# A hybrid decoder block: more matrix products by seven, two weight sums added by DMA, gate rows spread over two sweeps

## The chip, the cores and the metric

The kernel runs on one core of a Trainium2 chip. The metric is the device time of one execution in microseconds (us). The core has TensorE (matmuls, PE in the profile, with its weight loads as PEld), VectorE (DVE), ScalarE (ACT), GpSimd (POOL) and SyncE (SP), which issues nearly all transfers; 16 DMA engines move the bytes.

## The reference

One decoder block on 512 tokens of width 2048, in float32: adaLN modulation, an input projection, an RWKV-7 mixer beside a pooling mixer, an output projection, then a gated MLP with a causal convolution of width 3, and a final norm. What the change touches is the MLP and its last gate:

```python
def _conv_ffn(h, w_up, conv_w, conv_b, w_down):
    u = h @ w_up                                   # 2048 -> 2 * 5632
    up = jnp.pad(u, ((0, 0), (CONV_WIDTH - 1, 0), (0, 0)))
    y = conv_b
    for j in range(CONV_WIDTH):
        y = y + conv_w[j] * up[:, j:j + T]
    val, gate = jnp.split(y, 2, axis=-1)
    return (jax.nn.silu(gate) * val) @ w_down      # 5632 -> 2048

mod = c_act @ w_ada[l] + b_ada[l]
sh1, sc1, gt1, sh2, sc2, gt2 = jnp.split(mod[:, None, :], N_MOD, axis=-1)
...
x = x + gt2 * _conv_ffn(h, w_up[l], conv_w[l], conv_b[l], w_down[l])
```

## The kernel before, in words

Everything is held with features on the 128 partitions and the 512 tokens along the free dimension. A float32 product is made of three matmuls in a faster format: each operand is split into a high and a low part, and `mm3` does high x high, high x low and low x high (lines 121 to 123). ScalarE makes the high part by a cast, VectorE the low part by a difference. `split_weights` does so for a weight slice of 512 columns: it loads it into a `wraw` buffer (4 of them), casts to `whi`, subtracts to `wlo` (3 buffers, lines 113 to 117). `project` runs a row of such slices.

The program is traced in written order and ordered by a planner: it simulates the engines with estimated costs, gives each engine a fixed order of instructions, and lets a ready instruction go ahead of one written earlier that is not ready. Buffers are handed out in that simulated order too. On the chip each engine and each queue then runs its own list strictly in order and waits where data or a buffer is missing.

The MLP's inner width is 44 tiles of 128, and each comes as a pair, a value and a gate column block. Pairs 0 to 4 are done ordinarily. The next 26 pairs (`NSEV`) use a seven-product scheme on 2 x 2 blocks (value and gate, two halves of the tokens, two halves of the 2048 inputs). The inputs of a pair are cut into four chunks (`NPC`), and for each chunk the kernel loads four blocks of the weights (`load_four`, 512 KB), forms four sums of them on GpSimd (`weight_sums`: lines 956, 957, 958; the first writes two sums at once), splits three blocks and four sums into high and low parts (`parts`, lines 968 and 969: tiles ph, pl for the blocks, sh, sl for the sums, two buffers of each) and does seven products of six matmuls, each on half of the tokens: 42 matmuls of 128 x 256. Sums lie in buffers shared with the ordinary weights: two sums in a `wraw`, two in a `wlo`. The first three products use the blocks, the last four the sums. After the fourth chunk `combine` (lines 983 to 990) makes value and gate from the seven results; `gated` runs the convolution (lines 836 to 838), the gating (842, 843) and stores the tile to `actd`.

The 13 pairs that are left are done ordinarily, as a list of 104 quarters (`plain_tiles`): a quarter is one weight slice of 512 columns and 12 matmuls of 128 x 512, and every eighth ends a pair. One quarter is put between the two groups of products of each chunk from the third on; what remains runs after the last chunk.

The down projection then runs in two sweeps: eight output tiles at a time over all 44 inner tiles, four at a step. `act_tiles` loads and splits four tiles of `actd` (line 1065, 143, 144), and eight calls of `down` follow, each one weight slice and 12 matmuls. The last eight inner tiles of the second sweep are done by token halves together with the final norm. Before the down stage, 16 tiles of the residual are reloaded (line 1054) into a pool that takes the place of the up stage's own pool.

The gate of the MLP, 16 columns of the modulation, is computed on VectorE: `ada_gate2` loads a broadcast of a quarter of the activated `c` (line 1081) and rows of `w_ada` (256 KB each, line 1084, two buffers), and one VectorE instruction a row multiplies and sums (line 1085). 64 rows are needed, 16 columns times four quarters. They come in groups of eight, one group at each of steps 1 to 8 of the first sweep; at step 9 the quarters are added (lines 1094 to 1097).

Of the kernel before, what the change touches and what calls it, by code (L numbers as in the profile page):

```python
# [1 line left out]

# [1 line left out]

# [5 lines left out]
F32 = mybir.dt.float32  # L10
# [3 lines left out]
ALU = mybir.AluOpType  # L14
PSUM = bass.MemoryType.PSUM

P = 128
T = 512
D = 2048
KT = D // P  # L20
NF = 44
# [7 lines left out]
NB = 8  # L29
Q = float(np.exp(-0.5))  # L30
WINS = (2, 4, 8, 16)
NORD = 5
NSEV = 26
NPC = 4
DK = 4

# [26 lines left out]
def block_kernel(ctx, tc, a, out, stop=None, dbg=None):  # L63
    nc = tc.nc
    V, S, G, PE = nc.vector, nc.scalar, nc.gpsimd, nc.tensor
# [23 lines left out]
    def cols(name, lo, hi):  # L89
        return vec[:, COLS[name] + lo : COLS[name] + hi]  # L90
# [11 lines left out]
    mod = cp.tile([P, 96], F32, tag="mod", name="mod")  # L102
# [3 lines left out]
    V.tensor_scalar_add(b1p, cols("b_ada", 16, 32), 1.0)  # L106

    mark = [None, None]

    def split_weights(src, eng=V):  # L110
        w = src.shape[-1]
        raw = wp.tile([P, WC], F32, tag="wraw", name="wraw", bufs=4)
        nc.sync.dma_start(raw[:, 0:w], src)
        hi = wp.tile([P, WC], F32R, tag="whi", name="whi", bufs=3)
        mark[0] = S.copy(hi[:, 0:w], raw[:, 0:w]).ins  # L115
        lo = wp.tile([P, WC], F32R, tag="wlo", name="wlo", bufs=3)
        mark[1] = eng.tensor_tensor(lo[:, 0:w], raw[:, 0:w], hi[:, 0:w].bitcast(F32), op=ALU.subtract).ins  # L117
        return hi, lo

    def mm3(ps, wh, wl, xh, xl, start, stop):  # L120
        PE.matmul(ps, wh, xh, start=start, stop=False)  # L121
        PE.matmul(ps, wh, xl, start=False, stop=False)  # L122
        return PE.matmul(ps, wl, xh, start=False, stop=stop)  # L123

    def project(ps, src, acts, start=True, stop=True, engs=(V,)):

        n = len(acts)
        for k0 in range(0, n, WC // P):
            nk = min(WC // P, n - k0)
            wh, wl = split_weights(src[:, k0 * P : (k0 + nk) * P], engs[k0 // 4 % len(engs)])  # L130
            for kk in range(nk):
                k = k0 + kk
                sl = slice(kk * P, (kk + 1) * P)
                last = mm3(ps, wh[:, sl], wl[:, sl], *acts[k], start=start and k == 0, stop=stop and k == n - 1)
        return last

    def slots(k, tag="a"):
# [34 lines left out]
    cact = tc.dram_tile([1, D], F32, name="cact")  # L172
# [3 lines left out]
    first = {}  # L176
    p0ctx = ExitStack()
    p0 = p0ctx.enter_context(tc.tile_pool(name="p0", bufs=1))
    if True:
        cb = p0.tile([P, D], F32, tag="cb", name="cb")  # L180
# [29 lines left out]
        for k in range(KT):  # L210
# [7 lines left out]
            hi, lo = slots(k)  # L218
# [26 lines left out]
        for k in range(KT):  # L245
# [3 lines left out]
            hi, lo = slots(k)  # L249
# [465 lines left out]
    for g in range(NQ):  # L715
# [9 lines left out]
        if g < NQ - 1:  # L725
            win_some(pairs, (0, 2))
            with tc.high_priority(offset=50000):
                r, k = load_cells(g + 1, (0, 1))
# [50 lines left out]
    rb = ctx.enter_context(tc.tile_pool(name="rb", bufs=1, reuse_waits="tile"))  # L779
# [118 lines left out]
    upctx, up = stage("up")  # L898
# [33 lines left out]
    for j in range(2, NORD):  # L932
        tiles = []
        for i in range(2):
            ps = bank()
            last = project(ps, a["wup"][2 * j + i - 4, :, :], H2)
# [8 lines left out]

    W2 = 2 * P

    def load_four(n):
        raw = up.tile([P, 4, W2], F32, tag="raw", name="raw", bufs=2)
        nc.sync.dma_start(raw, a["wups"][n // NPC, n % NPC, :, :, :])  # L950
        return raw

    def weight_sums(raw):
        sa = wp.tile([P, WC], F32, tag="wraw", name="sums", bufs=4)[:, :].rearrange("p (n w) -> p n w", n=2)
        sb2 = wp.tile([P, WC], F32, tag="wlo", name="sums", bufs=3)[:, :].rearrange("p (n w) -> p n w", n=2)
        G.tensor_tensor(sa, raw[:, 1:3, :], raw[:, 0:1, :].to_broadcast([P, 2, W2]), op=ALU.add)  # L956
        G.tensor_tensor(sb2[:, 0, :], sa[:, 0, :], raw[:, 2, :], op=ALU.add)  # L957
        G.tensor_tensor(sb2[:, 1, :], sb2[:, 0, :], raw[:, 3, :], op=ALU.add)
        return sa, sb2

    def parts(tag, srcs):
        m = sum(t.shape[1] for t in srcs)
        hi = up.tile([P, m, W2], F32R, tag=tag + "h", name=tag + "h", bufs=2)
        lo = up.tile([P, m, W2], F32R, tag=tag + "l", name=tag + "l", bufs=2)
        n = 0
        for t in srcs:
            sl = slice(n, n + t.shape[1])
            act = S.copy(hi[:, sl, :], t)  # L968
            dve = V.tensor_tensor(lo[:, sl, :], t, hi[:, sl, :].bitcast(F32), op=ALU.subtract)  # L969
            n += t.shape[1]  # L970
        return [(hi[:, i, :], lo[:, i, :]) for i in range(m)], (act, dve)
# [21 lines left out]
    def plain_tiles():  # L993
        for j in range(NORD + NSEV, NF):
            yv = None
            for i in range(2):
                ps = bank()
                for k0 in range(0, KT, WC // P):
                    k1 = k0 + WC // P
                    project(ps, a["wup"][2 * (j - NSEV) + i - 4, :, k0 * P : k1 * P], H2[k0:k1],  # L1000
                            start=k0 == 0, stop=k1 == KT)
# [6 lines left out]

    NST = NSEV * NPC
    others = plain_tiles()  # L1010
    raws = [load_four(0), load_four(1)]
    sums = weight_sums(raws[0])
    pw, _ = parts("p", [raws[0][:, 1:4, :]])
    q = {}
    for n in range(NST):
        c = n % NPC
        if n + 1 < NST:
            raw = raws.pop()
            nsums = weight_sums(raw)
            npw, marks = parts("p", [raw[:, 1:4, :]])  # L1020
            if n + 2 < NST:
                raws.append(load_four(n + 2))
        with tc.issue_after(marks[0].ins), tc.issue_after(marks[1].ins):
            sw, _ = parts("s", sums)
        (a22, a11, a12), (s1, s3, s2, s4) = pw, sw
        ks = (2 * c, 2 * c + 1)
        b11, b21, b22 = half([H2[k] for k in ks], 0), half([H2[k + HK] for k in ks], 0), half([H2[k + HK] for k in ks], 1)
        t1, t2, t3, t4 = ([TK[k][i] for k in ks] for i in range(4))
        if c == 0:
            q = {}  # L1030
        for m, w, xs_ in ((1, a11, b11), (2, a12, b21), (4, a22, t4)):
            if c == 0:
                q[m] = bank()[:, 0:HT]
            product(q[m], c, w, xs_)
        if n >= 2:
            next(others, None)
        for m, w, xs_ in ((6, s2, t2), (7, s3, t3), (5, s1, t1), (3, s4, b22)):
            if c == 0:
                q[m] = bank()[:, 0:HT]
            product(q[m], c, w, xs_)  # L1040
        if c == NPC - 1:
            gated(NORD + n // NPC, *combine(q))
        if n + 1 < NST:
            sums, pw = nsums, npw
# [24 lines left out]
    def down(ps, f, k0, n, acts, start, stop):  # L1069
        project(ps, a["wdn"][f, :, k0 * P : (k0 + n) * P], acts, start=start, stop=stop)  # L1070
# [5 lines left out]

    modg = cp.tile([P, 4, KT], F32, tag="modg", name="modg")

    def ada_gate2(kq, js):
        cb = rb.tile([P, T], F32, tag="t0", name="cb2", bufs=2)  # L1080
        nc.sync.dma_start(cb, cact[0:1, kq * T : (kq + 1) * T].partition_broadcast(P))
        for j in js:
            wa = rb.tile([P, T], F32, tag="t1", name="wa3", bufs=2)
            nc.sync.dma_start(wa, a["ada3"][kq, j, :, :])
            V.scalar_tensor_tensor(wa, wa, 1.0, cb, op0=ALU.mult, op1=ALU.mult, accum_out=modg[:, kq, j : j + 1])  # L1085

    pss = [bank() for _ in range(NB)]
    for k0 in range(0, NF, DK):
        A = act_tiles(k0)
        n = k0 // DK  # L1090
        if 1 <= n <= 8:
            ada_gate2((n - 1) // 2, range(8 * ((n - 1) % 2), 8 * ((n - 1) % 2) + 8))
        if n == 9:
            V.tensor_add(modg[:, 0, :], modg[:, 0, :], modg[:, 1, :])
            V.tensor_add(modg[:, 2, :], modg[:, 2, :], modg[:, 3, :])
            V.tensor_add(modg[:, 0, :], modg[:, 0, :], modg[:, 2, :])
            V.tensor_add(mod[:, 80:96], modg[:, 0, :], cols("b_ada", 80, 96))
        for f in range(NB):
            down(pss[f], f, k0, DK, A, k0 == 0, k0 + DK == NF)
            if k0 + DK == NF:  # L1100
                residual(f, pss[f], gate(f), acc, 0, T, f == 0)
    pss = [bank() for _ in range(NB)]
    KL = NF - 2 * DK
    for k0 in range(0, KL, DK):
        A = act_tiles(k0)
        for f in range(NB):
            down(pss[f], NB + f, k0, DK, A, k0 == 0, k0 + DK == KL)
            if k0 + DK == KL:
                V.scalar_tensor_tensor(x2[NB + f], pss[f], gate(NB + f), x2[NB + f], op0=ALU.mult, op1=ALU.add)
    A = act_tiles(KL) + act_tiles(KL + DK)  # L1110
    for hf in range(2):
        for n in range(NB):
            f = NB + n
# [16 lines left out]
def pack(x, c, w_ada, b_ada, norm1_g, w_in, mu_shift, w0, w2, a0, a2, g2, k_k, k_a, r_k, ln_x_w, ln_x_b,  # L1130
# [49 lines left out]
    def ftiles(w):  # L1180
# [4 lines left out]
    wu = A(w_up[0]).reshape(D, 2, NF, P).transpose(0, 2, 1, 3).reshape(D, 88 * P)  # L1185
    n0, n1 = 2 * NORD * P, 2 * (NORD + NSEV) * P
    o["wup"] = ftiles(np.concatenate([wu[:, 4 * P : n0], wu[:, n1:]], 1))
    wq = wu[:, n0:n1].reshape(2, NPC, 2, P, NSEV, 2, P)
    o["wups"] = C(wq[(0, 1, 0, 1), :, :, :, :, (1, 1, 0, 0)].transpose(4, 1, 3, 0, 2, 5)).reshape(
        NSEV, NPC, P, 4, 2 * P)  # L1190
    o["wup0"] = C(wu[:, : 4 * P]).reshape(KT, P, 4 * P)
# [43 lines left out]
```

## Time and profile before

| | |
|---|---|
| median of three runs | 2365.94 us (2362.83 to 2372.0) |
| the profiled execution | 2367.17 us |
| its span, first to last instruction | 2365.4 us |
| TensorE busy | 2224.0 us, 94% |
| VectorE busy | 1512.8 us, 64% |
| ScalarE busy | 924.0 us, 39% |
| GpSimd busy | 404.7 us, 17% |
| HBM traffic over the span | 169 GB/s |
| mean granted clock of TensorE | 0.979 |

The span is the time between the first and the last recorded instruction of one execution; about 1.8 us of the execution lie around it. Busy times of the engines overlap. A matmul's row shows its duration in the pipeline, which is longer than the distance to the next one, so TensorE's pace is read from start times or counts. "What ended the idle time" in a row names the instruction or transfer that an engine last waited for.

### The profile page before, as it was taken

How to read it: one execution, taken by the hardware profiler on the slowest of the kernel's cores; microseconds unless marked ns; L12 is line 12 of the kernel's file. 1: busy time of each engine (PE TensorE's matmuls, PEld its weight loads, DVE VectorE, ACT ScalarE, POOL GpSimd, SP SyncE). 2: the span in 40 equal slices, each digit the busy share in tenths (PEclk: the TensorE clock that was granted, in tenths of full speed). 3: DMA queues.
4: the chain of work that ended last, by engine and by line, in shares of the span. 5: the costliest groups of instructions: out<-in, count | busy, mean ns of one | idle time of the engine just before them, and what ended most of it. 6: DMA issues, size and time to landing. Idle time of an engine off the chain costs nothing.

```text
span 2365.4 us, 41904 instructions
## 1 busy us (share of the span) xinstructions
PE 2224.0 (94%) x16306; PEld 1883.8 (80%) x16306; DVE 1512.8 (64%) x2532; ACT 924.0 (39%) x1551; POOL 404.7 (17%) x390
## 2 busy tenths in 40 slices
PE   7998888898979899999999999999999998999997
PEld 5776656665656798889999999999999766888886
DVE  7897667576876469766566666665666555353357
ACT  4335233242423255544434444444444322343333
POOL 0000000000000005643443343433342000000000
PEclk9999999999989999999999999999999999999998
DMA  9885555636775575533333333333334877555555
GB/s 349 301 305 170 157 188 164 205 117 206 226 225 163 179 225 169 148 115 109 116 121 115 113 121 108 116 116 113 109 115 133 272 242 231 148 152 143 143 164 179
DMA packets 197466, 401.42 MB, mean 170 GB/s; under 512 B 37521, under 2 KB 49553, under 8 KB 193041
## 3 DMA queue, kind: packets, MB, share of 16 engines
q1 hardware_dynamic: 197266, 398.73, 53.1%
q8 instruction: 128, 2.10, 0.4%
q14 instruction: 72, 0.59, 0.1%
HBM read 364.56 MB, written 34.09 MB: 169 GB/s over the span
## 4 chain that ended last, share of the span: by engine, by line
PE 48%; DMA 5%; DVE 2%; issue 1%; ACT 0%; SPq 0%; DVEq 0%; ACTq 0%
PE b L123 16%; PE b L121 16%; PE b L122 16%; DMA wa<-ada 2%; DMA ald<-actd 2%; DMA wraw<-wdn 1%; DVE wlo L117 1%; DVE wa L1085 0%; DVE x L1074 0%; DMA x<-x2d 0%; ACT ah L143 0%; DVE al L144 0%; ACT whi L115 0%; SPq L1054 0%; PE b L170 0%
## 5 line engine op out<-in xcount | busy, mean ns | idle before, releaser
L115 ACT CAST whi<-wraw 128x512 fp32r<-128x512 f32 (+1 forms) x594 | 360.1, 609 | 827.8 <-DMA wraw<-wup 264.6
L117 DVE TENSOR_TENSOR wlo<-wraw,whi 128x512 fp32r<-128x512 f32 (+1 forms) x578 | 406.0, 705 | 248.3 <-ACT whi L115 239.9
L123 PE MATMUL b<-ah,wlo 128*128 128x512 f32 (+1 forms) x980 | 352.6, 360 | 16.9 <-DVE wlo L117 15.9
L121 PE MATMUL b<-ah,whi 128*128 128x512 f32 (+1 forms) x980 | 351.3, 358 | 9.4 <-ACT whi L115 8.4
L122 PE MATMUL b<-al,whi 128*128 128x512 f32 (+1 forms) x980 | 349.5, 357 | 0.0
L123 PE MATMUL b<-hh,wlo 128*128 128x512 f32 (+1 forms) x640 | 237.4, 371 | 5.5 <-DVE wlo L117 5.4
L121 PE MATMUL b<-hh,whi 128*128 128x512 f32 (+1 forms) x640 | 237.7, 371 | 0.0
L122 PE MATMUL b<-hl,whi 128*128 128x512 f32 (+1 forms) x640 | 237.2, 371 | 0.0
L123 PEld LDWEIGHTS b<-ah,wlo 128*128 128x128 f32 x980 | 186.6, 190 | 53.2 <-DVE wlo L117 26.6
L121 PEld LDWEIGHTS b<-ah,whi 128*128 128x128 f32 x980 | 186.6, 190 | 38.6 <-ACT whi L115 13.7
L122 PEld LDWEIGHTS b<-al,whi 128*128 128x128 f32 x980 | 186.5, 190 | 26.4
L969 DVE TENSOR_TENSOR pl<-raw,ph 128x768 fp32r<-128x768 f32 x104 | 102.9, 989 | 153.6 <-ACT ph L968 153.6
L123 PE MATMUL mm<-ah,wlo 128*128 128x512 f32 x444 | 186.6, 421 | 6.6 <-DVE wlo L117 6.6
L121 PE MATMUL mm<-ah,whi 128*128 128x512 f32 x444 | 185.5, 418 | 7.2 <-ACT whi L115 6.6
L122 PE MATMUL mm<-al,whi 128*128 128x512 f32 x444 | 183.8, 414 | 0.0
L957 POOL TENSOR_TENSOR sums<-sums,raw 128x256 f32<-128x256 f32 x104 | 107.6, 1034 | 416.1 <-DVE sl L969 410.2
L123 PE MATMUL b<-tk,sl 128*128 128x256 f32 x624 | 176.7, 283 | 0.5 <-DVE sl L969 0.5
L122 PE MATMUL b<-tk,sh 128*128 128x256 f32 x624 | 176.6, 283 | 0.0
L121 PE MATMUL b<-tk,sh 128*128 128x256 f32 x624 | 176.1, 282 | 0.0
L372 DVE SCALAR_TENSOR_TENSOR war<-war,cq 128x1024 f32<-128x1024 f32 x96 | 117.2, 1222 | 85.5 <-DMA war<-ada 85.1
L968 ACT CAST ph<-raw 128x768 fp32r<-128x768 f32 x104 | 86.4, 831 | 164.4 <-PE b L122 157.8
L956 POOL TENSOR_TENSOR sums<-raw 128x512 f32<-128x512 f32 x104 | 137.7, 1324 | 67.9 <-DMA raw<-wups 36.3
(277 smaller groups left out, 4711.1 us busy)
## 6 DMA issues: line engine op xcount, KB each, us to landing
raw<-wups SPq DMA_DIRECT2D x104, 512.0 KB, 3.5
war<-ada SPq DMA_DIRECT2D x96, 512.0 KB, 4.3
wraw<-wdn SPq DMA_DIRECT2D x192, 256.0 KB, 3.1
wraw<-wup SPq DMA_DIRECT2D x160, 256.0 KB, 3.6
wa<-ada SPq DMA_DIRECT2D x32, 1024.0 KB, 7.7
wraw<-win SPq DMA_DIRECT2D x108, 256.0 KB, 4.1
ald<-actd SPq DMA_DIRECT2D x88, 256.0 KB, 2.8
wraw<-wout SPq DMA_DIRECT2D x78, 256.0 KB, 4.0
```

What stands on the lines that cost most here:

```text
L115: mark[0] = S.copy(hi[:, 0:w], raw[:, 0:w]).ins
L117: mark[1] = eng.tensor_tensor(lo[:, 0:w], raw[:, 0:w], hi[:, 0:w].bitcast(F32), op=ALU.subtract).ins
L121: PE.matmul(ps, wh, xh, start=start, stop=False)
L122: PE.matmul(ps, wh, xl, start=False, stop=False)
L123: return PE.matmul(ps, wl, xh, start=False, stop=stop)
L372: V.scalar_tensor_tensor(wa, wa, 1.0, cq[0], op0=ALU.mult, op1=ALU.mult, accum_out=modq[:, kq, j : j + 1])
L956: G.tensor_tensor(sa, raw[:, 1:3, :], raw[:, 0:1, :].to_broadcast([P, 2, W2]), op=ALU.add)
L957: G.tensor_tensor(sb2[:, 0, :], sa[:, 0, :], raw[:, 2, :], op=ALU.add)
L968: act = S.copy(hi[:, sl, :], t)
L969: dve = V.tensor_tensor(lo[:, sl, :], t, hi[:, sl, :].bitcast(F32), op=ALU.subtract)
```

## The change

There are three parts.

First, 32 pairs instead of 26 go by seven products, so that seven pairs, 56 quarters, are left for the ordinary way. A quarter is put into every fourth chunk (the last one of each pair), 32 in all; the other 24 run after the last chunk.

Second, the four weight sums of a chunk are made differently. The three blocks that are split are loaded as 384 KB (`load_three`). Two of these blocks are loaded a second time into the `wraw` buffer of the first two sums (`load_sums`, 256 KB, three chunks ahead), and a DMA issued by GpSimd adds the fourth block, read twice from HBM, onto them (`add_quarter`, up to two chunks ahead). GpSimd keeps the other two sums.

Third, the 64 gate rows are put one behind every second call of `down`, from the seventh call of the first sweep on: the first eight columns in the first sweep, the last eight in the second. A row is loaded one row ahead of its use, and its VectorE instruction is kept behind the last matmul of the `down` call that it follows in the planner's order (`in_step`, an order for the planner, not a wait on the chip). The quarters are added in two halves, after 32 and after 64 rows.

```diff
-NSEV = 26
+NSEV = 32
...
+    beats = []
+
+    def in_step(op, beat):
+        tc.add_manual_dep(op.ins, beat.name, mybir.DependencyInfo(mybir.DependencyClass.NoSync,
+                                                                  mybir.DependencyReason.DATA), reason="pace")
...  (project)
+            beats.append(last.ins)
...
-    def load_four(n):
-        raw = up.tile([P, 4, W2], F32, tag="raw", name="raw", bufs=2)
-        nc.sync.dma_start(raw, a["wups"][n // NPC, n % NPC, :, :, :])
+    def load_three(n):
+        raw = up.tile([P, 4, W2], F32, tag="raw", name="raw", bufs=2)[:, 0:3, :]
+        nc.sync.dma_start(raw, a["wups"][n // NPC, n % NPC, :, 1:4, :])
         return raw
 
-    def weight_sums(raw):
+    def load_sums(n):
         sa = wp.tile([P, WC], F32, tag="wraw", name="sums", bufs=4)[:, :].rearrange("p (n w) -> p n w", n=2)
+        nc.sync.dma_start(sa, a["wups"][n // NPC, n % NPC, :, 1:3, :])
+        return sa
+
+    def add_quarter(n, sa):
+        first = a["wups"][n // NPC, n % NPC, :, 0:1, :]
+        nc.gpsimd.dma_start(sa, first.to_broadcast([P, 2, W2]), accum_op=ALU.add)
+
+    def weight_sums(sa, raw):
         sb2 = wp.tile([P, WC], F32, tag="wlo", name="sums", bufs=3)[:, :].rearrange("p (n w) -> p n w", n=2)
-        G.tensor_tensor(sa, raw[:, 1:3, :], raw[:, 0:1, :].to_broadcast([P, 2, W2]), op=ALU.add)
-        G.tensor_tensor(sb2[:, 0, :], sa[:, 0, :], raw[:, 2, :], op=ALU.add)
-        G.tensor_tensor(sb2[:, 1, :], sb2[:, 0, :], raw[:, 3, :], op=ALU.add)
+        G.tensor_tensor(sb2[:, 0, :], sa[:, 0, :], raw[:, 1, :], op=ALU.add)
+        G.tensor_tensor(sb2[:, 1, :], sb2[:, 0, :], raw[:, 2, :], op=ALU.add)
         return sa, sb2
...
-    raws = [load_four(0), load_four(1)]
-    sums = weight_sums(raws[0])
-    pw, _ = parts("p", [raws[0][:, 1:4, :]])
+    raws = [load_three(0), load_three(1)]
+    sas = [load_sums(i) for i in range(3)]
+    add_quarter(0, sas[0])
+    add_quarter(1, sas[1])
+    sums = weight_sums(sas.pop(0), raws[0])
+    pw, _ = parts("p", [raws.pop(0)])
...
         if n + 1 < NST:
-            raw = raws.pop()
-            nsums = weight_sums(raw)
-            npw, marks = parts("p", [raw[:, 1:4, :]])
+            raw = raws.pop(0)
+            nsums = weight_sums(sas.pop(0), raw)
+            npw, marks = parts("p", [raw])
             if n + 2 < NST:
-                raws.append(load_four(n + 2))
+                raws.append(load_three(n + 2))
+                add_quarter(n + 2, sas[0])
+            if n + 3 < NST:
+                sas.append(load_sums(n + 3))
...
-        if n >= 2:
+        if n % 4 == 3:
             next(others, None)
...
-    def ada_gate2(kq, js):
-        cb = rb.tile([P, T], F32, tag="t0", name="cb2", bufs=2)
-        nc.sync.dma_start(cb, cact[0:1, kq * T : (kq + 1) * T].partition_broadcast(P))
-        for j in js:
-            wa = rb.tile([P, T], F32, tag="t1", name="wa3", bufs=2)
-            nc.sync.dma_start(wa, a["ada3"][kq, j, :, :])
-            V.scalar_tensor_tensor(wa, wa, 1.0, cb, op0=ALU.mult, op1=ALU.mult, accum_out=modg[:, kq, j : j + 1])
+    def ada_gate2(js):
+        loaded = []
+        for kq in range(4):
+            cb = rb.tile([P, T], F32, tag="t0", name="cb2", bufs=2)
+            nc.sync.dma_start(cb, cact[0:1, kq * T : (kq + 1) * T].partition_broadcast(P))
+            for j in js:
+                wa = rb.tile([P, T], F32, tag="t1", name="wa3", bufs=2)
+                nc.sync.dma_start(wa, a["ada3"][kq, j, :, :])
+                loaded.append((wa, cb, modg[:, kq, j : j + 1]))
+                if len(loaded) == 2:
+                    yield loaded.pop(0)
+        yield loaded.pop(0)
+
+    rows = itertools.chain(ada_gate2(range(NB)), ada_gate2(range(NB, KT)))
+
+    def gate_step(n):
+        if n % 2 or n < 6:
+            return
+        row = next(rows, None)
+        if row:
+            wa, cb, got = row
+            in_step(V.scalar_tensor_tensor(wa, wa, 1.0, cb, op0=ALU.mult, op1=ALU.mult, accum_out=got), beats[-1])
+        done = (n - 4) // 2
+        if done in (4 * NB, 4 * KT):
+            ...  (the four additions, for eight columns)
...  (first sweep)
-        n = k0 // DK
-        if 1 <= n <= 8:
-            ada_gate2((n - 1) // 2, range(8 * ((n - 1) % 2), 8 * ((n - 1) % 2) + 8))
-        if n == 9:
-            ...  (the four additions, for 16 columns)
         for f in range(NB):
             down(pss[f], f, k0, DK, A, k0 == 0, k0 + DK == NF)
+            gate_step(k0 // DK * NB + f)
...  (second sweep)
             down(pss[f], NB + f, k0, DK, A, k0 == 0, k0 + DK == KL)
+            gate_step((NF + k0) // DK * NB + f)
```

More of the change, by code (lines that the diff above doesn't have):

```diff
@@ L1 @@
 from contextlib import ExitStack
+import itertools
 import numpy as np
@@ L1077, in block_kernel @@
     modg = cp.tile([P, 4, KT], F32, tag="modg", name="modg")
-    def ada_gate2(kq, js):
-        cb = rb.tile([P, T], F32, tag="t0", name="cb2", bufs=2)
-        nc.sync.dma_start(cb, cact[0:1, kq * T : (kq + 1) * T].partition_broadcast(P))
-        for j in js:
-            wa = rb.tile([P, T], F32, tag="t1", name="wa3", bufs=2)
-            nc.sync.dma_start(wa, a["ada3"][kq, j, :, :])
-            V.scalar_tensor_tensor(wa, wa, 1.0, cb, op0=ALU.mult, op1=ALU.mult, accum_out=modg[:, kq, j : j + 1])
+    def ada_gate2(js):
[20 more added lines that the diff above has]
+        if done in (4 * NB, 4 * KT):
+            lo = done // 4 - NB
+            r = slice(lo, lo + NB)
+            V.tensor_add(modg[:, 0, r], modg[:, 0, r], modg[:, 1, r])
+            V.tensor_add(modg[:, 2, r], modg[:, 2, r], modg[:, 3, r])
+            V.tensor_add(modg[:, 0, r], modg[:, 0, r], modg[:, 2, r])
+            V.tensor_add(mod[:, 80 + lo : 80 + lo + NB], modg[:, 0, r], cols("b_ada", 80 + lo, 80 + lo + NB))
     pss = [bank() for _ in range(NB)]
@@ L1089, in block_kernel @@
         A = act_tiles(k0)
-        n = k0 // DK
-        if 1 <= n <= 8:
-            ada_gate2((n - 1) // 2, range(8 * ((n - 1) % 2), 8 * ((n - 1) % 2) + 8))
-        if n == 9:
[L1094 to L1097, printed above, removed]
         for f in range(NB):
             down(pss[f], f, k0, DK, A, k0 == 0, k0 + DK == NF)
+            gate_step(k0 // DK * NB + f)
             if k0 + DK == NF:
```

## The prediction

> **What bounds the kernel now.** I read the page first, then the stretches of the span by stage, then, inside the two stages that the change touches, groups, waits, SyncE's queue and the order of instructions.
>
> ```profile
> span 2365.4 us, 41904 instructions
> PE 2224.0 (94%) x16306; PEld 1883.8 (80%) x16306; DVE 1512.8 (64%) x2532; ACT 924.0 (39%) x1551; POOL 404.7 (17%) x390
> ```
>
> ```profile
> core 0: us, PE busy (x) PEld busy (x) DVE busy (x) ACT busy (x) POOL busy (x), PEclk, DMA share, GB/s
> 1136.00:1802.00 666.00, 666.00 (x4632) 624.29 (x4630) 411.64 (x654) 278.43 (x458) 265.24 (x258) 1.00 0.35 115
> 1836.00:1876.00 40.00, 37.34 (x157) 30.12 (x156) 19.23 (x38) 12.29 (x20) 0.00 (x0) 0.96 0.87 285
> 1876.00:2016.00 140.00, 125.81 (x523) 95.78 (x522) 80.32 (x183) 39.55 (x67) 0.00 (x0) 1.00 0.75 238
> 2036.00:2276.00 240.00, 240.00 (x1060) 198.79 (x1060) 99.49 (x148) 85.31 (x140) 0.00 (x0) 1.00 0.51 145
> ```
>
> TensorE bounds nearly everything. The first stretch is the seven-product stage: TensorE without a gap, VectorE 62% busy (411.64 of 666), 16 DMA engines at 0.35. There only fewer matmuls gain time. The fourth stretch is the second down sweep, also gapless: 1060 matmuls in 240 us, 4.42 per us. The third is the first down sweep with the gate rows in it; it does the same matmuls, but 523 in 140 us where that rate gives 618. So 95 are missing, 95 / 4.42 = 21.6 us of TensorE's time. The second stretch, the seam into the down stage, has 157 where 177 fit: 4.5 us.
>
> Busy time would read the third stretch as 140 - 125.81 = 14.2 us lost, the counts as 21.6. The Trainium skill ("Trainium Kernel Development and Optimization", Performance Expectations) calls matmul busy time a bad metric because matmuls are pipelined. The trace agrees (the missing 95 are seen in the counts only); by busy time the gain of the gate rows below would be some 7 us smaller.
>
> **Part 1, six more pairs with seven products.** One chunk in TensorE's order:
>
> ```profile
> 1400.31 0.28 PE L121 MATMUL b<-tk,sh 128*128 128x256 f32 x1
> ...
> 1405.34 0.40 PE L121 MATMUL b<-hh,whi 128*128 128x512 f32 x1
> ...
> 1408.09 0.28 PE L121 MATMUL b<-tk,sh 128*128 128x256 f32 x1
> ```
>
> From the first to the second row lie the 42 half-width matmuls of a chunk: 5.03 us, 0.12 each. From the second to the third lie the 12 of an ordinary quarter: 2.75 us. A pair done ordinarily is 8 quarters, 22.0 us; by seven products 4 chunks, 20.1 us. Six pairs change over: 48 x 2.75 - 24 x 5.03 = 132.0 - 120.7 = **11 us less**, if TensorE stays gapless. All 56 quarters that are left run somewhere: 32 between chunks, 24 in a row at the end (66 us), where a quarter asks 0.69 us of VectorE (row below), one load and 2.75 us of TensorE.
>
> Is the cover still there? Before, nearly every chunk had a quarter behind it (5.03 + 2.75 = 7.78 us); now three of four have none, so a chunk has 5.03 us and a pair 4 x 5.03 + 2.75 = 22.9 us.
>
> ```profile
> L956 POOL TENSOR_TENSOR sums<-raw 128x512 f32<-128x512 f32 x102 | 135.1, 1324 | 51.0 <-DMA raw<-wups 36.3 <-DVE u L987 5.9 <-issue 4.6
> L969 DVE TENSOR_TENSOR sl<-sums,sh 128x512 fp32r<-128x512 f32 x200 | 132.8, 704 | 0.0
> L968 ACT CAST sh<-sums 128x512 fp32r<-128x512 f32 x200 | 113.7, 616 | 0.0
> L957 POOL TENSOR_TENSOR sums<-sums,raw 128x256 f32<-128x256 f32 x102 | 105.8, 1037 | 404.1 <-DVE sl L969 404.0
> L969 DVE TENSOR_TENSOR pl<-raw,ph 128x768 fp32r<-128x768 f32 x100 | 99.1, 991 | 144.7 <-ACT ph L968 144.7
> L958 POOL TENSOR_TENSOR sums<-sums,raw 128x256 f32<-128x256 f32 x102 | 75.5, 740 | 8.0
> L117 DVE TENSOR_TENSOR wlo<-wraw,whi 128x512 fp32r<-128x512 f32 x99 | 68.4, 691 | 0.1
> L843 DVE TENSOR_TENSOR t<-t,t 128x512 f32<-128x512 f32 x37 | 34.4, 930 | 9.1 <-ACT t L842 9.1
> L837 DVE SCALAR_TENSOR_TENSOR t<-cv,vec,t 128x511 f32<-128x511 f32 x24 | 18.0, 751 | 0.0
> L984 DVE TENSOR_TENSOR cv<-cg,b 128x256 f32<-128x256 f32 x25 | 10.5, 421 | 91.8 <-PE b L123 72.4 <-ACT cg L983 19.4
> ```
>
> VectorE per pair: four chunks of one 0.99 and two 0.70, 9.6; combining 7 x 0.42 = 2.9; the convolution 4 x 0.75 + 0.93 = 3.9; an ordinary quarter 0.69, and a pair's 3.9 over eight quarters, 0.5. Sum 17.6 of 22.9 us: 77%, up from 62%. It fits on average. Whether it fits behind a pair's end, where combining and convolution come in one lump, the order there tells:
>
> ```profile
> 1395.78 0.41 DVE L989 TENSOR_TENSOR cv<-u,b 128x256 f32<-128x256 f32 x1
> 1398.62 0.75 DVE L837 SCALAR_TENSOR_TENSOR t<-cg,vec,t 128x511 f32<-128x511 f32 x1 [2.43 <-ACT t L836]
> ...
> 1401.31 0.95 DVE L969 TENSOR_TENSOR pl<-raw,ph 128x768 fp32r<-128x768 f32 x1
> 1402.18 0.68 DVE L843 TENSOR_TENSOR t<-t,t 128x512 f32<-128x512 f32 x1
> 1402.78 1.28 DVE L969 TENSOR_TENSOR sl<-sums,sh 128x512 fp32r<-128x512 f32 x2
> ```
>
> L989 reads the pair's last product, so TensorE finished the pair at about 1395.7. The first of the two sl is done at 1403.4, 7.7 us later. In the new order TensorE has, after a pair's end, 18 + 24 + 18 = 60 matmuls, 7.2 us, until it asks for these sl: 0.5 us too late if nothing shifts. But 2.43 us of the 7.7 VectorE sat waiting for ScalarE, which was held by a weight cast whose load was late; without this the sl come 1.9 us early. So the stall is between 0 and 32 x 0.5 = 16 us; I take **+6**, a third, since the lone 2.43 decides.
>
> **Part 2, sums by accumulating DMA.** POOL loses L956, 1.32 us a chunk, and keeps 1.04 + 0.74 = 1.78. It gains the issue of one DMA a chunk; SyncE gains a 256 KB load a chunk, and a 384 KB load takes the place of 512 KB. TensorE never waited for POOL here, so the lost 1.32 us gains nothing by itself. SyncE issues in 0.33 us (below), so one more is free. No row shows a DMA issued from POOL or one that adds. Its issue I bound by SyncE's 0.33 and by the POOL row that it replaces, 1.32: take 1.0, nearer a POOL row. Its landing by other transfers:
>
> ```profile
> 1402.33 0.33 SPq L950 DMA_DIRECT2D raw<-wups  x1
> ```
>
> ```profile
> raw<-wups SPq DMA_DIRECT2D x104, 512.0 KB, 3.5
> wa<-ada SPq DMA_DIRECT2D x32, 1024.0 KB, 7.7
> x<-x2d SPq DMA_DIRECT2D x16, 256.0 KB, 4.7
> out<-x SPq DMA_DIRECT2D x32, 128.0 KB, 1.8
> ```
>
> So 1.8 to 7.7 us; I take 4, near the 512 KB row, as it reads source and destination of 256 KB. A sum's way is then load 3.5, issue 1, landing 4, POOL 1.78, two casts 1.2, two differences 1.4: 12.9 us. It holds one of four wraw buffers, of which an ordinary quarter takes about one in five: 3.2 x 5.72 us (22.9 / 4) = 18.3 us. It fits with 5 us to spare; a landing of 7.7 still fits. The traffic, 384 + 256 + 256 KB with some 128 KB beside them each 5.72 us, is 183 GB/s, and with the destination read 229; the seam ran at 285. Cost **0**, from -1 (no wait gone) to the rival's price below. The first chunk now waits for two transfers in a row rather than one; TensorE has ordinary work ahead of it: **+1** (0 to 4).
>
> At the seam, the last 66 us use none of the stage's own buffers, so the 16 reloads of 256 KB can start under them instead of all at once: of the 4.5 us I take **-2** (0 to -4).
>
> **Part 3, gate rows over both sweeps.** Why the 21.6 us are lost:
>
> ```profile
> SPq L1084 <- DVE wa L1085: 49.7, 49, 3.1
> SPq L113 <- DVE al L144: 11.7, 16, 1.4
> ```
>
> ```profile
> PEld b L123 <- DVE wlo L117: 20.6, 21, 1.9
> ACT ah L143 <- DMA ald<-actd: 57.1, 20, 6.8
> ```
>
> Rows come eight at a time with two buffers, so SyncE stands 49.7 us in front of a row's load until VectorE has used up the row before, and the weight and activation loads queued behind it start late; TensorE then waits for VectorE's split. The edit issues one row in two down steps (24 matmuls, 5.4 us at 4.42 per us), its load a row ahead. A row lands in a few us, so SyncE finds its buffer free. Nothing is removed: 64 rows, eight broadcasts and 0.77 us of VectorE a row stay, and half of them move to the second sweep, where VectorE is 99.49 of 240 us busy and DMA at 145 GB/s; a row each 5.4 us adds 48, 193 in all, below the 238 of the third stretch. Hidden there: 0 (up to 4.5, what the seam lost at 285). In the first sweep I take **-20** (-14 to -21.6); late next is the activation load of each four tiles.
>
> **Sum.** -11 + 6 + 0 + 1 - 2 - 20 = -26. Against the profiled execution's own 2367.17 (span 2365.4 and 1.8 around it, 1.2 over the median 2365.94): **2341 us**.
>
> **Rivals.**
> (B) The pair's end becomes the bound. The ordinary weight's load gets its wraw buffer later than now, as sums hold buffers longer, and ScalarE, in order, holds the convolution behind its cast for a microsecond more.
>
> ```profile
> ACT whi L115 <- DMA wraw<-wup: 254.7, 70, 5.6
> ```
>
> For it: ScalarE waits 3.6 us a time here already. Price 0.5 + 1.0 = 1.5 us a pair, 48 in place of 6: 2383, slower. It decides from 1.0 us a pair (32 us, the sum without the stall). Against it: only one chunk in four has such a cast, and that one is 7.78 us long.
> (C) POOL becomes the bound. Written order on POOL is the sums of one chunk, the next one's accumulation, that one's sums. Kept so, a chunk costs 1.78 + issue + landing: 1.78 + 1.0 + 4.0 = 6.8 us (3.9 to 10.8) against 5.72; 128 x 1.1 = 138 more in place of 6: 2473. It decides from 6.0 us a chunk. Against it: above, the planner put pl of a later chunk ahead of L843, which is written first, so it fills an idle engine; the next accumulation then goes ahead of the waiting sums. The Trainium skill ("DMA: Bandwidth & Descriptors", Anatomy of one DMA — SWDGE (gpsimd) path) gives 2.0 us plus the bytes at 436 GB/s for a plain POOL-issued DMA, an estimated 2.6 us for 256 KB; by it the chunk is 5.4 us and (C) does not decide. No run here shows it.
> (D) The rows cost the same wherever they lie, as when the transfers themselves and not the queue hold TensorE: half the loss stays and half moves. Then -6 without -20: 2361. Against it: SyncE's wait above names VectorE, not a DMA.
>
> **How the numbers follow.** Forecast 0.64 (its own range 2328 to 2354: stall 0 to 16, seam 0 to -4, rows -17 to -21.6), B 0.12, C 0.14, D 0.10. Two runs of this kernel differ by up to 0.4%, so 0.5% (11.8 us: 2354 and 2378) is what can be told from no change. Faster 0.60 (the forecast less its edge); same 0.16 (that edge 0.04, D, 0.02 of B); slower 0.24 (B, C). The range 2326 to 2388 takes in all but C and a little at the edges.
>
> **What would show it.** Right: bare chunks 5.03 us apart with TensorE gapless; POOL's accumulation issued ahead of the waiting sums; SyncE's wait for the row before gone from its queue's waits; over 600 matmuls in the 140 us after the seam. Wrong: TensorE waiting for sl behind every fourth chunk (B); even spacing above 5.72 us with POOL waiting for the accumulating transfer (C); the first sweep faster and the second slower (D). A landing far above 7.7 us would break the prediction.

## The result, and the profile after

| kernel | median | against before, same chip |
|---|---|---|
| before | 2367.8 us | |
| changed | 2447.0 us (2431.6 to 2450.5) | 1.0325 (1.0295 to 1.0356), +79 us |

The changed kernel is 3.3% slower; 2341 was forecast, 2326 to 2388 as the range. The page of the profile after, its span, engines and queues:

```profile
span 2445.8 us, 43219 instructions
PE 2250.1 (92%) x16738; PEld 1930.4 (79%) x16738; DVE 1549.9 (63%) x2602; ACT 952.4 (39%) x1581; POOL 448.5 (18%) x462
...
q1 hardware_dynamic: 212242, 415.52, 53.8%
q0 software_dynamic: 34816, 33.56, 9.5%
```

TensorE's share fell from 94% to 92%, and no other engine is near its limit. The stretches of the span (columns as before the change) show where:

```profile
1022.00:1868.00 846.00, 772.86 (x5716) 744.16 (x5715) 512.92 (x811) 347.07 (x555) 363.57 (x382) 0.95 0.65 160
1920.00:1960.00 40.00, 40.00 (x178) 33.13 (x177) 20.34 (x30) 17.00 (x28) 0.00 (x0) 1.00 0.60 172
1960.00:2100.00 140.00, 140.00 (x619) 115.97 (x618) 67.67 (x129) 45.99 (x75) 0.00 (x0) 1.00 0.66 201
2120.00:2360.00 240.00, 240.00 (x1060) 198.79 (x1060) 121.44 (x224) 85.94 (x141) 0.00 (x0) 1.00 0.62 185
```

The last three stretches are the seam and the two down sweeps: 178 matmuls in 40 us (157 before), 619 in 140 us (523 before), 1060 in 240 us (as before, with 32 rows more in it). The first is nearly all of the stage of 128 chunks. By start times the stage runs from 1027.9 to 1877.5 us: 850 us, where 128 x 5.03 + 32 x 2.75 = 732 would do. Some 117 us are lost there, with the granted clock at 0.95 (1.00 before). What TensorE waited for in that stretch, and SyncE's queue (selected rows; waited for: us in total, times, longest):

```profile
PEld b L128 <- ACT whi L122: 76.7, 31, 3.9
PE b L128 <- ACT whi L122: 70.4, 31, 3.7
```

```profile
SPq L958 <- DVE pl L984: 500.4, 124, 6.4
SPq L963 <- DVE sl L984: 79.9, 84, 3.1
SPq L120 <- DVE sl L984: 7.2, 7, 2.6
```

L122 is the cast of the ordinary quarter's weights, L120 their load; L958 and L963 load the blocks and the sums. There are 32 quarters between chunks, and TensorE waits 2.3 us for the cast at 31 of them. The chain of waits around two of them (start, us, what):

```profile
1416.49 0.84 ACT ph L983
1417.39 0.84 issue
1418.23 0.69 DVE sl L984
1418.94 5.32 DMA wraw<-wup
1424.29 0.63 ACT whi L122
1424.96 0.50 PE b L128
...
1443.30 0.69 DVE sl L984
1444.01 5.55 DMA wraw<-wup
1449.59 0.63 ACT whi L122
1450.26 0.50 PE b L128
...
1452.62 0.21 PE b L129
1452.84 0.43 PE b L130
1453.26 0.43 PE b L128
1453.69 0.43 PE b L129
```

Read from the bottom of each group: the quarter's first matmul waits for the cast, the cast for the load, and the load was issued 0.02 us after the first difference sl ended (1418.23 + 0.69, or 1443.30 + 0.69), the instruction that gives a wraw buffer back. The load takes 5.3 to 5.6 us, and TensorE has only 3.95 us of work left when it is issued. It is so at all 32 loads: each is issued within 0.05 us behind the end of an sl.

The kernel before had the same release. Its lines:

```profile
1446.06 1.28 DVE L969 TENSOR_TENSOR sl<-sums,sh 128x512 fp32r<-128x512 f32 x2
...
1446.77 0.33 SPq L113 DMA_DIRECT2D wraw<-wup  x1
...
1450.45 0.62 ACT L115 CAST whi<-wraw 128x512 fp32r<-128x512 f32 x1 [4.26 <-DMA wraw<-wup]
...
1452.02 0.40 PE L121 MATMUL b<-hh,whi 128*128 128x512 f32 x1
```

There too the load goes just behind the first of two sl (so it is at 73 of 98 loads of that stage), but TensorE has 5.25 us of work left, the load lands in a median of 3.7 us, and the cast is done a median of 1.0 us ahead of the matmul. In the changed kernel the load lands in a median of 5.5 us and 1.3 us of the time for it are gone.

After the second pause the clock fell to half for 3.4 us: matmuls of 0.23 us take 0.43, and some 1.6 us are lost once more.

Start-to-start distances of all matmuls between 1060 and 1780 us, less 0.12 us for 256 columns and 0.2285 for 512, add up what is lost in each kernel (worked out from the trace's start times):

| us lost in 720 | in pauses over 1 us | under 0.3 us (slow clock, mostly) | in all |
|---|---|---|---|
| changed | 64.7 (27) | 28.0 (220) | 95 |
| gate rows alone | 0 | 0 | 0 |

### The profile page after: what moved, and what is told of

It is laid out like the page before. It is cut to its first block, busy times and chain, and to the rows that moved or that the text cites. A ratio compares the mean times of both kernels' runs of the same rounds, so it can differ in the third digit from the quotient of the medians.

```text
span 2445.8 us, 43219 instructions
## 1 busy us (share of the span) xinstructions
PE 2250.1 (92%) x16738; PEld 1930.4 (79%) x16738; DVE 1549.9 (63%) x2602; ACT 952.4 (39%) x1581; POOL 448.5 (18%) x462
## 3 DMA queue, kind: packets, MB, share of 16 engines
q0 software_dynamic: 34816, 33.56, 9.5%
## 4 chain that ended last, share of the span: by engine, by line
PE 63%; DMA 17%; DVE 10%; issue 4%; ACT 4%; SPq 1%; POOL 0%; DVEq 0%; ACTq 0%; POOLq 0%
PE b L128 17%; PE b L129 16%; PE b L130 16%; DMA wraw<-wup 7%; DMA war<-ada 4%; PE mm L130 2%; PE mm L129 2%; PE mm L128 2%; DVE wlo L124 2%; PE pf L128 1%; DVE war L380 1%; DMA wa<-ada 1%; ACT whi L122 1%; PE pf L129 1%; PE pf L130 1%
## 5 line engine op out<-in xcount | busy, mean ns | idle before, releaser
L124 DVE TENSOR_TENSOR wlo<-wraw,whi 128x512 fp32r<-128x512 f32 (+2 forms) x530 | 378.4, 717 | 356.9 <-ACT whi L122 341.8
L122 ACT CAST whi<-wraw 128x512 fp32r<-128x512 f32 (+2 forms) x546 | 330.3, 608 | 675.9 <-PE b L129 278.9
L128 PE MATMUL b<-hh,whi 128*128 128x512 f32 (+1 forms) x448 | 173.5, 387 | 70.4 <-ACT whi L122 70.4
L130 PE MATMUL b<-tk,sl 128*128 128x256 f32 x768 | 222.6, 291 | 2.3 <-DVE sl L984 2.3
L984 DVE TENSOR_TENSOR pl<-raw,ph 128x768 fp32r<-128x768 f32 x128 | 125.9, 983 | 155.0 <-ACT ph L983 155.0
L129 PE MATMUL b<-tk,sh 128*128 128x256 f32 x768 | 222.5, 290 | 0.0
L128 PE MATMUL b<-tk,sh 128*128 128x256 f32 x768 | 222.2, 290 | 0.0
L983 ACT CAST ph<-raw 128x768 fp32r<-128x768 f32 x128 | 106.7, 834 | 240.0 <-PE b L129 226.2
L130 PE MATMUL b<-hh,wlo 128*128 128x512 f32 (+1 forms) x448 | 171.1, 382 | 6.9 <-DVE wlo L124 6.9
L984 DVE TENSOR_TENSOR sl<-sums,sh 128x512 fp32r<-128x512 f32 x256 | 168.8, 698 | 3.7 <-ACT sh L983 3.7
L129 PE MATMUL b<-hl,whi 128*128 128x512 f32 (+1 forms) x448 | 169.2, 378 | 0.0
```

## The experiments

Differences are to the kernel before on the same chip; three-round comparisons have an interval, the others are one run each.

| | sums made by | buffers for sums and quarters | quarter behind | us against before |
|---|---|---|---|---|
| changed | adding DMA | 4 | 4th chunk | +79 |
| own | adding DMA | 4 + 1 for quarters | 4th | +60 |
| queue | adding DMA | 4 | 4th | +92 |
| noacc | GpSimd | 4 | 4th | -15 |
| rows (26 pairs) | GpSimd | 4 | every | -24 |
| ring7 | adding DMA | 7 shared | 4th | -1 |
| plain | copying DMA | 4 | 4th | +14 |
| acc26 (26 pairs) | adding DMA | 4 | every | +103 |
| ring7plain | copying DMA | 7 shared | 4th | -22 |
| noacc2 | GpSimd | 4 | 2nd | -19 |
| ring7s | adding DMA | 7 shared | 2nd | -21 |

**The third part alone (rows).** The kernel before with `ada_gate2`, `gate_step` and `in_step` of the change and nothing else of it.

> The kernel before with only the third part, the gate rows over both sweeps. By the traces (523 against 619 matmuls in the 140 us of the first sweep, and 1060 in 240 us of the second sweep in both kernels): about 21 us faster than before, 2346 us; with the rows' cost only moved: 2362 to 2368.

2344.8 us, 0.9899 (0.9867 to 0.9932), 23.6 us faster. The gate rows do what was forecast, and the loss lies in the other two parts. SyncE's wait in front of a row's load, 57.4 us in 57 waits before, is nearly gone (both between 1836 and 2016 us):

```profile
SPq L1095 <- DVE wa L1109: 6.9, 30, 0.3
```

**Without the DMA-made sums (noacc).** `load_four` and the three-instruction `weight_sums` put back into the changed kernel.

> The changed kernel without its second part: blocks come by one 512 KB load and GpSimd makes all four sums, so a wraw buffer is taken by a sum only when GpSimd starts on it. Theory 1 (buffer): the quarter's load comes early again, 2330 to 2360 us. Theory 2 (queue): the block loads stand in SyncE's queue as before it, 2420 to 2450. Theory 3 (pace): 2420 to 2450. Theory 4 (slow accumulating DMA): 2330 to 2345.

2353.6 us, 0.994 (0.9917 to 0.9964). Theories 2 and 3, the queue and the pace, had 2420 to 2450 here and fall; theory 1's range holds, theory 4's 2330 to 2345 is missed by 9 us. 93 us go with the second part of the change. The first part costs 9 us over the gate rows alone, and its remaining waits are those of the pair's end (waits between 1060 and 1800 us, as in the runs below unless said):

```profile
PEld b L130 <- DVE sl L977: 24.9, 34, 2.1
PE b L130 <- DVE sl L977: 17.8, 31, 1.9
```

The two rows are one wait, seen once at the weight load and once at the matmul. Here a quarter's load is issued a median of 10.5 us ahead of its matmuls, against 6.2 in the changed kernel with the wait in it.

**The load's queue (queue).** The edit, shortened:

```diff
-        nc.sync.dma_start(raw[:, 0:w], src)
+        loader[0].dma_start(raw[:, 0:w], src)     # ScalarE's queue for quarters between chunks
```

> The changed kernel, but the load of each quarter between chunks is issued from ScalarE's queue, with the same buffers. Theory 1 (buffer): unchanged, 2430 to 2455 us, or worse as ScalarE now stands waiting for the buffer. Theory 2 (SyncE's queue): 2330 to 2360. Theories 3 and 4: unchanged.

2460.5 us: no better. In the changed kernel the load stands right behind a block load in SyncE's queue, so the queue could have set its time; on ScalarE's queue it still goes within 0.05 us behind the end of an sl, at all 32 loads. The buffer holds it, not the queue.

```profile
1419.63 1.29 DVE L986 TENSOR_TENSOR sl<-sums,sh 128x512 fp32r<-128x512 f32 x2
...
1420.35 0.33 ACTq L122 DMA_DIRECT2D wraw<-wup  x1
```

**A buffer for the quarters (own).** The edit, shortened:

```diff
-        raw = wp.tile([P, WC], F32, tag="wraw", name="wraw", bufs=4)
+        raw = up.tile([P, WC], F32, tag="wown", name="wown", bufs=1)     # quarters between chunks only
```

> The changed kernel, but the ordinary weights between chunks get a buffer of their own (the blocks' two buffers shrink from 4 to 3 KB a partition to make room; the token sums use other buffers for that). The changed kernel's stage of 128 chunks takes 846 us where its matmuls need 128 x 5.03 + 32 x 2.75 = 732: 114 us lost, about 70 in which TensorE waits for the quarter's cast and 42 by a granted clock of 0.95. Theory 1 (buffer: the quarter's load waits until a sum gives up one of the four wraw buffers): the waits go and the clock returns to 1.00, 2330 to 2345 us. Theory 2 (queue: it stands in SyncE's queue behind a load of blocks that waits for a free buffer): its place in the queue moves up too, so also 2330 to 2345. Theory 3 (pace: three bare chunks leave VectorE and ScalarE too little time whatever the buffers): 2420 to 2450. Theory 4 (the accumulating DMA is too slow): 2420 to 2450.

2428.8 us, 1.0256 (1.0222 to 1.0291): only 18 us of the expected 100. TensorE no longer waits for the cast, but for sums at the pair's end, and SyncE for GpSimd's sums:

```profile
PE b L135 <- DVE sl L989: 51.6, 29, 3.0
```

```profile
SPq L963 <- POOL sums L978: 383.9, 92, 8.8
SPq L963 <- DVE pl L989: 204.5, 92, 8.0
```

The quarter's buffer is single, and its next load can only go when the quarter's low part is made: it goes 0.03 to 1.5 us behind that. ScalarE then stands in front of the next cast (77.9 us in 28 waits for the load), and the sums' casts stand behind it. This run alone would have spoken for theories 3 and 4.

**Seven shared buffers (ring7).**

```diff
-        sa = wp.tile([P, WC], F32, tag="wraw", name="sums", bufs=4)...
+        sa = wp.tile([P, WC], F32, tag=("wraw", "whi")[n % 2], name="sums", bufs=(4, 3)[n % 2])...
```

> The changed kernel, but every second pair of DMA-made sums lies in the three buffers of the weights' high parts, of which only one quarter in four chunks makes use, so sums and ordinary weights share seven buffers rather than four; no buffer is added and no other tile moves. The run with one buffer of its own for the quarter's weights gave 2428.8 us: TensorE no longer waited for the quarter's cast, but for the sums' low parts at each pair's end, with ScalarE's order held at the quarter's cast. Theory 1 (too few buffers for the sums' ring and the quarter's weights together): 2340 to 2365 us. Theory 4 (the way over two transfers and POOL is too long by itself, whatever the buffers): 2400 to 2450 us, with POOL's sums waiting for the adding DMA.

2363.4 us, 0.9986 (0.9967 to 1.0006): 84 us off the changed kernel's median. A quarter's load now goes a median of 20 us ahead of its matmuls (one of them below), TensorE's waits for its cast are gone, and the pair's end is left, as without DMA-made sums:

```profile
1222.81 0.37 SPq L120 DMA_DIRECT2D wraw<-wup  x1
...
1244.45 0.40 PE L128 MATMUL b<-hh,whi 128*128 128x512 f32 x1
```

```profile
PE b L130 <- DVE sl L984: 17.3, 18, 2.4
```

GpSimd still waits for the adding DMA (179 us in 47 waits between 1060 and 1800 us), and TensorE's waits for sl are no longer in sum than without such DMAs (17.8 us). Theory 1 stands, though not for everything: against the kernel before this run is 14 us worse than the one without DMA-made sums.

**The addition itself (plain).**

```diff
-        nc.gpsimd.dma_start(sa, first.to_broadcast([P, 2, W2]), accum_op=ALU.add)
+        nc.gpsimd.dma_start(sa, first.to_broadcast([P, 2, W2]))
```

> The changed kernel with GpSimd's DMA copying in place of adding (the quarter overwrites the two sums, so the products are of other weights); each queue's order of instructions is the same as in the changed kernel. It prices the addition in the DMA. If adding in the transfer is what is slow (theory 4a): the landing falls from a median of 4.7 to 3 us or less and the time by 20 us or more, to 2425 or below. If the time lies in the order, the buffers and the number of transfers: 2435 to 2455 us.

2378.4 us, 69 us off, with the same order on every queue and the same four buffers. By its time the addition is what is slow; the landing fell to 3.9 us and not to 3, and from 6.4, not from the 4.7 of the expectation. Transfers by line of the changed kernel (KB each, median us to landing), then of this one, and its queues:

```profile
raw<-wups SPq DMA_DIRECT2D x128, 384.0 KB, 4.5
sums<-wups SPq DMA_DIRECT2D x128, 256.0 KB, 4.2
sums<-wups POOLq DMA_DIRECT2D x128, 256.0 KB, 6.4
```

```profile
raw<-wups SPq DMA_DIRECT2D x128, 384.0 KB, 3.4
sums<-wups SPq DMA_DIRECT2D x128, 256.0 KB, 3.3
sums<-wups POOLq DMA_DIRECT2D x128, 256.0 KB, 3.9
...
q0 software_dynamic: 10240, 33.56, 4.9%
```

The adding transfer lands in 6.4 us instead of 3.9, in 34816 packets instead of 10240 and with twice the share of the DMA engines (9.5% against 4.9%), and the plain loads beside it land a microsecond later. GpSimd's issue takes 1.2 us instead of 0.72. Between 1060 and 1800 us the quarters' own loads land in a median of 5.5 us in the changed kernel, 4.2 here. A quarter still waits here, but about 1.1 us:

```profile
PE b L128 <- ACT whi L122: 34.3, 30, 2.1
```

So a load that lands 1.3 us sooner takes 1.1 us off each wait, and the clock, 0.95 in the changed kernel, is back at 1.00 between 1136 and 1802 us. By start times 41 us are lost in the 720 instead of 95, and no stretch at half clock is left.

**The cover back (acc26).** `NSEV = 26`, and a quarter behind each chunk from the third on.

> The changed kernel with 26 pairs and a quarter behind each chunk from the third on, as before: the kernel with the gate rows alone (2344.8 us) plus the DMA-made sums. Theory 1 (buffers): a quarter behind each chunk asks for a buffer each 7.8 us beside three sums in four, so TensorE waits at nearly every quarter: 2400 us or more. Theory 3 (without the cover of a quarter per chunk the DMA-made sums come too late): with the cover back, 2340 to 2355 us.

2467.5 us, as theory 1 had it: a quarter per chunk is no cover but one more claim on the four buffers. TensorE waits for the cast 27 times (60.9 us), though, not at nearly every quarter.

```profile
ACT whi L122 <- DMA wraw<-wup: 371.1, 82, 8.7
POOL sums L968 <- DMA sums<-wups: 275.0, 40, 10.0
```

```profile
SPq L963 <- DMA wraw<-wup: 333.2, 83, 6.4
```

The sums' loads (L963) stand until a quarter's load has landed, 83 times, and ScalarE stands in front of the quarter's cast.

**Both edits (ring7plain).**

> Both of the last two edits at once, seven buffers for sums and quarters' weights and a GpSimd DMA that copies in place of adding (so other weights enter the products). Seven buffers alone took 84 us off the changed kernel, copying alone 69. If both relieve the same wait, the quarter's late load: no more than 10 us below seven buffers alone, 2350 to 2365 us. If they are two costs that add: 2447 - 84 - 69 = 2294, and in any case below 2330.

2346.0 us. 84 and 69 do not add to 153; together they take 101, a little more than the 94 that was the expectation's edge. They relieve largely the same wait. What more buffers don't relieve and a quicker transfer does is some 17 us (21 with each run set against the kernel before on its own chip).

**The spacing, without (noacc2) and with DMA-made sums (ring7s).** `if n % 2 == 1:` for `if n % 4 == 3:`.

> The changed kernel without the DMA-made sums (2353.6 us), and with a quarter behind every second chunk in place of every fourth, 56 of 56 quarters between the first 112 chunks. There TensorE waited about 43 us in all for the sums' low parts behind pairs' ends, where three bare chunks follow one another. If that lump is what ate the 11 us that six more pairs should save: the waits go and it comes to the kernel with gate rows alone less 11, 2330 to 2340 us. If not, 2350 or more, as GpSimd's 3.1 us a chunk or VectorE's load bind whatever the spacing.

2349.5 us, 0.9914 (0.9881 to 0.9947). The waits for sums at pairs' ends fell from 17.8 us to 6.6 (between 1030 and 1830 us), yet it missed 2330 to 2340. The 43 us of the expectation counts one wait twice, at the weight load and at the matmul:

```profile
PE b L130 <- DVE sl L977: 6.6, 10, 1.6
```

By start times it loses 5.7 us in the 720 and about 6 between 1780 and 1860, where its last chunks run bare; that is most of the 16 us between it and the kernel with gate rows alone less 11. A part of some microseconds is not found.

> The changed kernel with seven buffers for sums and quarters' weights and a quarter behind every second chunk in place of every fourth. Seven buffers alone gave 2363.4 us; there TensorE still waited for sums' low parts behind pairs' ends. A quarter behind every second chunk took 4 us off the kernel without DMA-made sums (2349.5). If GpSimd's time is what kept that one above the kernel with gate rows alone (2344.8): 2332 to 2342 us, as the DMA-made sums relieve GpSimd. If the adding DMA costs in itself whatever the buffers (its packets take twice the engine time, and the quarters' loads land later): 2350 to 2365, or worse, as twice as many quarters' loads stand beside it.

2345.1 us, 0.9909 (0.9877 to 0.9941). It misses its 2332 to 2342 by 3 us, is 18 us below seven buffers alone, and level with the gate rows alone (0.9899). Both beat the kernel before and the changed one by about 1% and 4%; six more pairs brought nothing measurable over the gate rows in any form tried. In this last one some 7 of the 11 us are found by start times: 5 more than in the gate rows alone are lost between 1015 and 1060 us, where the first sums wait for two transfers, and 2 in the 720. With all quarters between the chunks it has no ordinary run at the end either, and the seam has 157 matmuls in 40 us as before.

## Why the prediction was wrong

- **Part 2, cost 0: the step that failed.** The check of the buffers, 12.9 of 18.3 us, was made for the sums alone. It counted the quarter as one more tenant ("about one in five"), Part 1 priced it as "one load", and nothing asked which release gives that load its buffer and how long before its matmuls. It is an sl that ends 3.95 us of TensorE's work ahead of them, and the load and cast then need 6.2. Before, the same release left 5.25 us and 4.4 were needed: the cover was one microsecond, and the change took it twice, by 1.3 us less work in between and by a load of 5.5 us in place of 3.7 beside the new transfers. Price: 2.3 us of waiting and about 1 us of slow clock at each of 31 quarters.
- **Its landing was mis-sized too.** The adding DMA was taken as 4 us, nearest the 512 KB row; it was 6.4, inside the bounds of 1.8 to 7.7, and its issue 1.2 against 1.0. By the prediction's own check that still fits (15.5 of 18.3 us), so the check, not only the size, was at fault. For a plain DMA from GpSimd the prediction estimated 2.6 us; copying, it took 3.9.
- **Part 1, the saving of 11 us: right in TensorE's work, wrong in what is kept.** The stall at the pair's end was put at 6 within 0 to 16. Without DMA-made sums it is seen: waits for sl of 17.8 us, and 9 us net loss against the gate rows alone where the saving should show, so some 20 by the medians (28 us by start times in the 720, part of which the relieved seam gives back). The term was mis-sized by three or more; the lone 2.43 us of ScalarE was not the rule. One reason it did not have: of the sl in that run, the 71 beside one of GpSimd's sums last 1.23 us (median), those alone 0.68; in the kernel before 5 of 200 fell beside one. How much of the stall this makes is not shown.
- **The first chunk, +1 within 0 to 4: too small.** Between 1015 and 1049 us the changed kernel loses 4.6 us, the gate rows alone 0.7. That is the upper edge; with seven buffers (ring7) 9.1 are lost there.
- **Part 3, gate rows: right.** -20 was forecast within -14 to -21.6; the sweep's matmul count went to the full rate (-21.6 by the counts), nothing came back in the second sweep, and alone it measured -23.6, a little past the edge and within its interval. Reading the loss off counts, not busy time (14.2), was right. Rival D falls.
- **The seam: right in kind, a little short.** -2 was forecast within 0 to -4; 178 matmuls against 157 in 40 us is -4.75, just past the edge. That it comes from the 24 quarters at the end is borne out: without them (quarters behind every second chunk) it is 157 again.
- **Rival B named the buffer and the place and had the wrong waiter.** It had the quarter's load late "as sums hold buffers longer", but made ScalarE's convolution the victim at 1.5 us a pair. TensorE itself waited for the quarter, 3.5 us a pair with the clock. That put the time at 2383 and not at 2447.
- **Rival C did not happen.** The planner did issue accumulations in pairs ahead of the waiting sums, as argued (two of L968 in a row at 1405.99 us), and GpSimd's waits for the transfer hardly reached TensorE (2.3 us of waits for sl). By the rival's own sum, with the measured 1.2 and 6.4, a strict order would have cost 9.4 us a chunk against 5.72.
- **The clock was in no term.** It took 28 of the 95 us lost in the 720.
- **The range of the forecast alone** comes out of its terms as about 2331 to 2356, not 2328 to 2354. It changes nothing.

## What to carry to other kernels

A ring of buffers that several streams share is priced for each stream: write down which release gives the rarer stream its buffer, and how long before its use that comes. A prefetch that starts earlier holds its buffer longer; and a stream that was in time by one microsecond is starved as soon as its load lands two microseconds later. When one edit's relief and another's overlap (84 and 69 gave 101), both attack one wait.

## What the runs showed of the hardware

- Adding in the transfer is dear: for the same 33.56 MB, 34816 packets against 10240, 9.5% against 4.9% of the 16 engines, 6.4 against 3.9 us to land, and other loads a microsecond later. With seven buffers it is less: 5.9 against 4.7 us to land, and other loads 0.2 to 0.3 us later.
- The row of a GpSimd-issued DMA lasts 1.20 us when adding and 0.72 when copying. The next sum on GpSimd can start within the row, so it is not shown that GpSimd is held for all of it.
- The clock fell to half after short pauses. Of the changed kernel's pauses between 1060 and 1800 us (start to start of two matmuls), none of the 6 up to 2.0 us was followed by slow matmuls and 18 of the 22 longer ones were, mostly for about 1.5 us of loss; without the addition no pause exceeded 2.4 us and none was. The Trainium skill ("TensorE: Matmul & The Clock Gate", HAM oscillation — how this bites in real kernels) warns of TensorE idle for more than about 3.4 us; in this trace 2.04 us sufficed once, and 2.90 did not once.
- Length alone does not decide. Between 1060 and 1800 us the trace's records of the granted clock are at 0.5 for 3.41 us at a time (twice for 6.83), and all begin on one grid of 3.41 us. Laid on that grid, the 18 stretches ahead of a fall hold 1.9 us of pause or more, and the 10 others with over 1 us, at full clock, hold 1.1 to 1.8. In the other runs the border lies between 1.8 and 2.0. Two pairs of stretches of the grid show it (columns as above, the clock third from the end): the pause of 2.42 us lies all in one, the one of 2.90 us is cut in two.

```profile
1447.28:1450.69 3.41, 1.27 (x9) 1.03 (x9) 1.74 (x3) 1.25 (x4) 1.43 (x2) 1.00 0.92 194
1450.69:1454.11 3.42, 3.42 (x14) 3.03 (x13) 2.44 (x7) 0.55 (x2) 0.00 (x0) 0.50 0.60 190
1576.99:1580.40 3.41, 1.86 (x16) 1.65 (x14) 1.52 (x3) 0.83 (x1) 1.11 (x2) 1.00 0.78 179
1580.40:1583.82 3.42, 2.35 (x14) 2.12 (x15) 1.89 (x5) 1.66 (x3) 0.00 (x0) 1.00 0.59 158
```
